# GpSimd in the mixing stage: decay products, probability normalisation and one weight cast per layer

## The chip, the cores and the metric

The kernel runs on one core of one Trainium2 chip. The metric is device time in microseconds, the median of several runs. Engines are named as in the profile: PE is TensorE, DVE is VectorE, ACT is ScalarE, POOL is GpSimd, SP is SyncE, which issues most of the DMAs.

## The reference

Two layers of a decoder trunk over 256 tokens of width 1024, in f32. A layer is half a SwiGLU, a mixing step with three branches, another half SwiGLU and a per-layer embedding; a norm ends the program. The change lies in mixing:

```
u  = rmsnorm(h);  u @ w_in is split among three branches and three gates
A) sparse attention:   logits = q . c_sel * 64**-0.5, masked to the top 64 keys of each query
                       probs  = softmax(logits);  out = probs @ c_sel @ w_uv
B) pooling mixer:      trailing means over 2/4/8/16 tokens minus the token itself, a 128x128 map per group
C) SSD, 2 chunks of 128 tokens, 16 heads in 2 groups:
                       L      = exp(segsum(A))                      (decay within a chunk)
                       y_diag = (C_l . B_s * L[l, s]) @ X           per head
                       ... states, y_off, skip, gate, norm
h += (sum_b sigmoid(gate_b) * (branch_b @ w_b)) @ w_out
```

## The kernel before

Weights come in units of 128 x 1024 f32, each stored so that eight 128 x 128 blocks follow each other. SP loads a unit into `raw` (4 buffers), ACT casts it to a high part `whi` (L145; 5 buffers), DVE subtracts to get the low part `wlo` (L146; 5 buffers), and PE multiplies in three passes, high by high, high by low and low by high (L211 to L213), into a PSUM bank named `mm` (products of weight units) or `aux` (everything else). Units are asked for up to four ahead.

In `mix` the branches are Python generators that `weave` interleaves: `states` (the SSD branch), `attend` (attention), `pools` (pooling) and `gate` (the gate projections, which fill PE in between; `U_IN` + 45 is one of their units). A scheduler then orders each engine's instructions by a timeline of its own, so an edit on one engine can move rows on others; engines wait for each other by semaphores, and each runs its queue in order.

The names that matter: `ms` (tile `ct` in the profile) holds the decays of a chunk `h` and a group `g`, 8 heads as two halves of 4 x 128. DVE makes a running sum of the rates (`rates`, loaded by DMA to tile `gh`) with a scan (L1099), ACT takes the exponential (L1104), for `h == 0` DVE copies the last column to `e0` (L1107), and L1108 multiplies by `cb` (tile `gl`), the product of B and C that all heads of a group share. `near` (helper line L111) multiplies the result with X on PE. In `softmax`, `ps` holds the logits of 4 heads x 128 keys (`h == 0`, one pair of tiles) or 2 heads x 256 keys (`h == 1`, two calls with a pair each); DVE adds the mask and finds the maximum (L921), ACT takes the exponential and its sum (L923), DVE the reciprocal (L925), ACT multiplies each head by its own (L927), PE transposes `pr` (tile `t2`, helper line L114), ACT copies the transposed tile (L939). In `pool_group`, DVE adds shifted copies (L1168, L1169), corrects the start (L1173), takes the mean minus the token (L1176), ACT casts to a high part (L1181) and DVE, or GpSimd for the third group, subtracts for the low part (L1183). GpSimd also scales X by dt (L1085), masks the index scores (L893) and, at the end of the program, scales a gain (L1258). L260 is the low part of a scaled split, and L1031 a step of dt.

Of the kernel before, what the change touches and what calls it, by code (L numbers as in the profile page):

```python
# [13 lines left out]
OP = mybir.AluOpType  # L14
AX = mybir.AxisListType

P = 128
# [38 lines left out]
U_IN = U_KV + 2  # L56
# [12 lines left out]
class Builder:  # L69
# [71 lines left out]
    def load(self, layer, u, n, keep=False):  # L141
        nc = self.nc
        raw, hi, lo = self.parts()
        nc.sync.dma_start(raw[:, :n], self.ins["w"][layer, u, :, :n])
        nc.scalar.copy(hi[:, :n], raw[:, :n])  # L145
        ins = nc.vector.tensor_tensor(lo[:, :n], raw[:, :n], hi[:, :n].bitcast(F), op=OP.subtract)  # L146
        if keep:
            self.tc.keep_in_program_order(ins)
        self.turn(ins)
        return hi, lo  # L150
# [757 lines left out]
    def softmax(self, h, two, mb, out):  # L908

        nc = self.nc  # L910
        nb = h + 1
        nk = nb * P
        per = 512 // nk
        prs = []
        for ps, _ in two:
            pr = self.t([P, per, nk])
            mx = self.t([P, per], tag="mx", bufs=2)
            sums = self.t([P, per], tag="sum", bufs=2)
            for j in range(per):
                x = mx[:, j:j + 1]  # L920
                nc.vector.tensor_tensor_reduce(pr[:, j], ps[:, j * nk:(j + 1) * nk], mb[:, :nk],  # L921
                                               1.0, 3.0e38, OP.add, OP.min, accum_out=x)
                self.last = nc.scalar.activation(pr[:, j], pr[:, j], AF.Exp, bias=x, scale=-1.0,  # L923
                                                 accum_out=sums[:, j:j + 1])
            nc.vector.reciprocal(sums, sums)  # L925
            for j in range(per):
                nc.scalar.mul(pr[:, j], pr[:, j], sums[:, j:j + 1])  # L927
            prs.append(pr)
            yield
        for _ in range(4 - h):  # L930
            yield
        pts = [self.bank("aux") for _ in prs]
        for pt, pr in zip(pts, prs):
            for j in range(4):
                self.transpose(pt[:, j * P:(j + 1) * P],
                               pr[:, j // nb, (j % nb) * P:(j % nb + 1) * P], self.ident)
        for (_, heads), pt in zip(two, pts):
            th = self.t([P, 4, P])
            nc.scalar.copy(th, pt.rearrange("p (a b) -> p a b", a=4))  # L939
            out.append((heads, th))  # L940
            yield
# [63 lines left out]
    def ssd(self, layer, sm, xs, xt, bc, cb, zs, room):  # L1005
        nc = self.nc
# [53 lines left out]
        def rate(*key):  # L1060
            i = wanted.index(key)
            for k in wanted[i:i + 3]:
                if k not in rates:
                    rates[k] = fetch(*k)
            return rates[key]
# [26 lines left out]
        for g in range(2):  # L1092
            gs = slice(g * 4, (g + 1) * 4)
            for h in range(2):
                ms = self.a([P, 2, 4, P], F, "ct")
                for q in range(2):

                    m = ms[:, q]
                    nc.vector.tensor_tensor_scan(m.rearrange("p a b -> p (a b)"),  # L1099
                                                 rate(g, h, q).rearrange("p a b -> p (a b)"),  # L1100
                                                 self.after.rearrange("p a b -> p (a b)"),
                                                 0.0, OP.add, OP.mult)
                    yield
                    self.last = nc.scalar.activation(m, m, AF.Exp)  # L1104
                    if h == 0:
                        k = g * 8 + q * 4
                        nc.vector.tensor_copy(e0[:, k:k + 4], m[:, :, P - 1])  # L1107
                    nc.vector.tensor_tensor(m, m, cb[:, h, g, None].to_broadcast([P, 4, P]),  # L1108
                                            op=OP.mult)
                    yield  # L1110
                ps = self.bank("aux")

                def near():
                    for j in range(8):
                        b, k = (j % 2) * 64, j // 2
                        self.mm(ps[b:b + 64, k * P:(k + 1) * P],
                                         xt[:, h, g * 8 + j], ms[:, j // 4, j % 4],
                                         start=True, stop=True)

                yield  # L1120
                yield
                yield near
                yk = y[:, gs, h * P:(h + 1) * P]
                nc.vector.tensor_tensor(yk, yk, ps.rearrange("p (a b) -> p a b", a=4), op=OP.add)
                yield

            x0 = self.t([P, 8, 64])
            nc.vector.tensor_tensor(x0, xt[:, 0, g * 8:(g + 1) * 8],
                                    e0[:, g * 8:(g + 1) * 8, None].to_broadcast([P, 8, 64]),
                                    op=OP.mult)  # L1130
            po = self.bank("aux")
            e1 = self.t([P, 4, P])
            x = rate(g, 1, 2)
            for j in range(4):
                nc.vector.tensor_tensor_scan(e1[:, j], x[:, j], self.ones, 0.0, OP.add, OP.mult)
            self.last = nc.scalar.activation(e1, e1, AF.Exp)
            yield
            yield
            for j in range(4):
                a = x0[:, 2 * j:2 * j + 2].rearrange("p a b -> p (a b)")  # L1140
                self.mm(po[:, j * P:(j + 1) * P], a, cb[:, 2, g], start=True, stop=True)
            yield
            nc.vector.tensor_tensor(e1, po.rearrange("p (a b) -> p a b", a=4), e1, op=OP.mult)
            yk = y[:, gs, P:]
            nc.vector.tensor_tensor(yk, yk, e1, op=OP.add)
            yield
            if g == 0:
                ysh, ysl = [], []
            ysh.append(self.a([P, 4, S], FR, "a4", 7))
            ysl.append(self.a([P, 4, S], FR, "a4", 7))  # L1150
            for i in range(4):
                k = g * 4 + i
                nc.vector.tensor_tensor(y[:, k], y[:, k], zs[:, k], op=OP.mult)
                self.square(k, y[:, k])
                self.split_scaled(ysh[g][:, i], ysl[g][:, i], y[:, k],
                                  self.col(layer, "ssd_norm", k))
                yield
# [336 lines left out]
```

## Time and profile before

| what | before |
|---|---|
| median of 3 runs | 1299.63 us (1299.38 to 1300.03) |
| the profiled execution | 1300.84 us, of which the span of instructions is 1299.1 us |
| PE busy | 1290.3 us (99%) |
| DVE busy | 1046.3 us (81%) |
| ACT busy | 739.5 us (57%) |
| POOL busy | 17.9 us (1%), 27 instructions |
| mixing of layer 0, woven part | about 290 to 370 us |
| mixing of layer 1, woven part | about 935 to 1015 us |

Busy time of PE counts from a matmul's start to its modelled end, and matmuls overlap; a wait shows as a gap between starts. In the views below a row of the timeline is start, duration, engine, line, operation, result and inputs by the program's names; a group's row ends with busy time, the mean in ns and idle time before it. Line numbers are those of the kernel before; in the changed kernel they are 3 higher from L146 on up to the normalisation and 2 higher behind it.

### The profile page before, as it was taken

To read this page: it belongs to the slowest core of one execution; us is meant where nothing else is said; L and a number is where in the kernel's file an instruction comes from. 1 tells how busy PE (TensorE), PEld (TensorE's weight loads), DVE (VectorE), ACT (ScalarE), POOL (GpSimd) and SP (SyncE) were. 2 spreads that over 40 slices of the span, in tenths; PEclk is the share of its full clock that TensorE was granted. 3 is DMA by queue.
4 is the path that set the end of the run, shared out by engine and by line. 5 is a ranking of instruction groups with operands and counts; after the bars stand their busy time and mean duration, and the time that the engine had idled before them with its cause. 6 is when DMAs were issued, how large, how long until landed. Compare 5 with 4: busy or idle time off the path is not lost.

```text
span 1299.1 us, 28286 instructions
## 1 busy us (share of the span) xinstructions
PE 1290.3 (99%) x11398; PEld 1282.0 (99%) x11398; DVE 1046.3 (81%) x1935; ACT 739.5 (57%) x1209; POOL 17.9 (1%) x27
## 2 busy tenths in 40 slices
PE   9999999999999999999999999999999999999998
PEld 9999999999999999999999999999999999999998
DVE  7877669987999887766997776799879989777667
ACT  6644446666874555544654444476667646544455
POOL 0000000000000000000000000000100000000000
PEclk9999999999999999999999999999999999999999
DMA  7766646586647576666556665556965566655661
GB/s 251 247 193 195 194 158 211 179 222 205 188 142 235 162 227 194 195 191 194 188 195 194 194 196 191 162 192 184 212 224 165 183 199 211 197 195 193 194 194 66
DMA packets 89571, 250.51 MB, mean 193 GB/s; under 512 B 25184, under 2 KB 27872, under 8 KB 89440
## 3 DMA queue, kind: packets, MB, share of 16 engines
q1 hardware_dynamic: 89008, 247.92, 60.6%
q8 instruction: 89, 1.46, 0.5%
q10 hardware_dynamic: 432, 0.79, 0.2%
q14 instruction: 42, 0.34, 0.1%
HBM read 245.50 MB, written 1.08 MB: 190 GB/s over the span
## 4 chain that ended last, share of the span: by engine, by line
PE 87%; DVE 7%; ACT 2%; DMA 2%; issue 2%; DVEq 0%; SPq 0%; ACTq 0%
PE mm L213 27%; PE mm L212 27%; PE mm L211 27%; DVE wlo L146 2%; DVE ct L1099 1%; PE aux L111 1%; ACT whi L145 1%; DMA gh<-rates 1%; DMA raw<-in_w_dram 1%; PE mm L230 1%; PE mm L227 1%; PE aux L213 1%; PE aux L212 1%; ACT t L923 1%; PE mm L225 1%
## 5 line engine op out<-in xcount | busy, mean ns | idle before, releaser
L145 ACT CAST whi<-raw 128x1024 fp32r<-128x1024 f32 (+1 forms) x456 | 475.1, 1045 | 484.9 <-PE mm L212 353.8
L146 DVE TENSOR_TENSOR wlo<-raw,whi 128x1024 fp32r<-128x1024 f32 (+1 forms) x456 | 552.2, 1215 | 170.1 <-ACT whi L145 162.2
L212 PE MATMUL mm<-ul,whi 128*128 128x256 f32 x2438 | 672.0, 276 | 0.0
L213 PE MATMUL mm<-uh,wlo 128*128 128x256 f32 x2438 | 671.8, 277 | 0.0
L211 PE MATMUL mm<-uh,whi 128*128 128x256 f32 x2402 | 662.3, 277 | 0.8 <-ACT whi L145 0.8
L212 PEld LDWEIGHTS mm<-ul,whi 128*128 128x128 f32 x2438 | 457.5, 188 | 0.1
L213 PEld LDWEIGHTS mm<-uh,wlo 128*128 128x128 f32 x2438 | 457.0, 188 | 0.2
L211 PEld LDWEIGHTS mm<-uh,whi 128*128 128x128 f32 x2402 | 449.8, 188 | 2.1 <-ACT whi L145 1.2
L213 PE MATMUL mm<-gh,wlo 128*128 128x256 f32 x704 | 194.1, 276 | 0.0
L212 PE MATMUL mm<-gl,whi 128*128 128x256 f32 x704 | 194.1, 276 | 0.0
L211 PE MATMUL mm<-gh,whi 128*128 128x256 f32 x704 | 193.7, 276 | 0.0
L213 PEld LDWEIGHTS mm<-gh,wlo 128*128 128x128 f32 x704 | 132.2, 188 | 0.0
L212 PEld LDWEIGHTS mm<-gl,whi 128*128 128x128 f32 x704 | 132.2, 188 | 0.0
L211 PEld LDWEIGHTS mm<-gh,whi 128*128 128x128 f32 x704 | 131.9, 188 | 0.0
L212 PE MATMUL mm<-a,whi 128*128 128x256 f32 x256 | 70.7, 276 | 0.0
L213 PE MATMUL mm<-a,wlo 128*128 128x256 f32 x256 | 70.7, 276 | 0.0
L211 PE MATMUL mm<-a,whi 128*128 128x256 f32 x256 | 70.7, 276 | 0.0
L213 PEld LDWEIGHTS mm<-a,wlo 128*128 128x128 f32 x256 | 48.1, 188 | 0.0
L211 PEld LDWEIGHTS mm<-a,whi 128*128 128x128 f32 x256 | 48.1, 188 | 0.0
L212 PEld LDWEIGHTS mm<-a,whi 128*128 128x128 f32 x256 | 48.1, 188 | 0.0
L498 DVE TENSOR_TENSOR t<-mm,rs_r 128x256 f32<-128x256 f32 x88 | 37.3, 424 | 13.2 <-PE mm L213 13.0
L499 DVE TENSOR_TENSOR t<-t,mm 128x256 f32<-128x256 f32 x87 | 36.5, 420 | 2.6
(300 smaller groups left out, 1271.1 us busy)
## 6 DMA issues: line engine op xcount, KB each, us to landing
raw<-in_w_dram SPq DMA_DIRECT2D x446, 512.0 KB, 4.3
gh<-rates SPq DMA_DIRECT2D x16, 256.0 KB, 4.1
raw<-in_w_dram SPq DMA_DIRECT2D x8, 352.0 KB, 3.0
ul<-a SPq DMA_DIRECT2D x32, 64.0 KB, 4.8
a<-in_x_dram SPq DMA_DIRECT2D x3, 512.0 KB, 5.3
gh<-rates SPq DMA_DIRECT2D x8, 128.0 KB, 4.5
a<-in_x_dram SPq DMA_DIRECT2D x1, 544.0 KB, 3.7
raw<-in_w_dram SPq DMA_DIRECT2D x2, 256.0 KB, 4.4
```

The costliest lines, as they stand in the source:

```text
L111: self.tc.keep_in_program_order(self.nc.tensor.matmul(*args, **kw))
L145: nc.scalar.copy(hi[:, :n], raw[:, :n])
L146: ins = nc.vector.tensor_tensor(lo[:, :n], raw[:, :n], hi[:, :n].bitcast(F), op=OP.subtract)
L211: (self.mm if keep else mm)(ps, a[0], b[0], start=start, stop=False)
L212: mm(ps, a[0], b[1], start=False, stop=False)
L213: mm(ps, a[1], b[0], start=False, stop=stop)
L225: (self.mm if keep and k == 0 else mm)(ps, w[0][:, s], u[0][:, k], start=k == 0, stop=False)
L227: mm(ps, w[0][:, s], u[1][:, k], start=False, stop=False)
L230: mm(ps, w[1][:, k * P:(k + 1) * P], u[0][:, k], start=False, stop=k == last)
L498: ins = [nc.vector.tensor_tensor(t, p1[0], r, op=OP.mult), nc.vector.tensor_tensor(g, t, p1[1], op=OP.mult)]
L499: nc.vector.tensor_tensor(g, t, p1[1], op=OP.mult)]
L923: self.last = nc.scalar.activation(pr[:, j], pr[:, j], AF.Exp, bias=x, scale=-1.0, accum_out=sums[:, j:j + 1])
```

## The change

Three pieces of mixing go to GpSimd. The decay products change their engine and keep their shape (128 x 512). The normalisation becomes one product of 128 x 512 with the reciprocals broadcast along the keys, for each tile of probabilities, in place of one ACT instruction per head. And one weight unit per layer, `U_IN` + 45, is cast on GpSimd.

```diff
@@ load
         nc.sync.dma_start(raw[:, :n], self.ins["w"][layer, u, :, :n])
-        nc.scalar.copy(hi[:, :n], raw[:, :n])
+        if u == U_IN + 45:
+            nc.gpsimd.tensor_copy(hi[:, :n], raw[:, :n])
+        else:
+            nc.scalar.copy(hi[:, :n], raw[:, :n])
@@ softmax
             nc.vector.reciprocal(sums, sums)
-            for j in range(per):
-                nc.scalar.mul(pr[:, j], pr[:, j], sums[:, j:j + 1])
+            nc.gpsimd.tensor_tensor(pr, pr, sums[:, :, None].to_broadcast([P, per, nk]), op=OP.mult)
             prs.append(pr)
@@ ssd
                         nc.vector.tensor_copy(e0[:, k:k + 4], m[:, :, P - 1])
-                    nc.vector.tensor_tensor(m, m, cb[:, h, g, None].to_broadcast([P, 4, P]),
+                    nc.gpsimd.tensor_tensor(m, m, cb[:, h, g, None].to_broadcast([P, 4, P]),
                                             op=OP.mult)
```

The scheduler's order changes with it. On GpSimd the following stood before from layer 0's product with dt on (`ul_541` and `t1_683` belong to mixing of layer 0, `gl_1585` and `ul_1780` to layer 1):

```order
L1085 TENSOR_TENSOR ul_541_3872<-ul_541_3872,dt_547_3902 128x512 x4
L1183 TENSOR_TENSOR t1_683_4786<-t1_681_4783,t1_682_4785 128x256
L893 AFFINE_SELECT gl_1585_11072<-gl_1585_11072 128x128 x2
L1085 TENSOR_TENSOR ul_1780_12469<-ul_1780_12469,dt_1786_12499 128x512 x4
L1258 TENSOR_SCALAR idxw_2450_17030<-idxw_2450_17030 128x256
```

Now its queue reads as follows behind the same product of layer 0 (`ct_589` and `ct_610` are decays of the first group, `ct_669` and `ct_691` of the second, chunk 0 ahead of chunk 1; `t2_601` to `t2_704` tiles of probabilities, `whi_613` the unit's high part):

```order
L1110 TENSOR_TENSOR ct_589_4170<-ct_589_4170,gl_346_2475 128x512 x2
L1110 TENSOR_TENSOR ct_610_4314<-ct_610_4314,gl_346_2475 128x512 x2
L146 CAST whi_613_4323<-raw_612_4322 128x1024
L929 TENSOR_TENSOR t2_601_4268<-t2_601_4268,sum_603_4270 128x512
L929 TENSOR_TENSOR t2_607_4301<-t2_607_4301,sum_609_4303 128x512
L1110 TENSOR_TENSOR ct_669_4709<-ct_669_4709,gl_346_2475 128x512 x2
L929 TENSOR_TENSOR t2_647_4564<-t2_647_4564,sum_649_4566 128x512
L929 TENSOR_TENSOR t2_657_4614<-t2_657_4614,sum_659_4616 128x512
L1185 TENSOR_TENSOR t1_683_4778<-t1_681_4775,t1_682_4777 128x256
L1110 TENSOR_TENSOR ct_691_4845<-ct_691_4845,gl_346_2475 128x512 x2
L929 TENSOR_TENSOR t2_692_4849<-t2_692_4849,sum_694_4851 128x512
L929 TENSOR_TENSOR t2_704_4897<-t2_704_4897,sum_706_4899 128x512
```

Every decay product, every normalisation and the cast of layer 0 stand in one queue, the pooled group's subtraction among them.

PE at the last softmax of layer 0 (`aux_718` takes the first tile's transposes, `aux_719` the second's, `mm_714` is a gate projection, `mm_721` the fourth pooled group), before:

```order
L212 MATMUL mm_714_4970<-ul_389_2714,whi_678_4746 128x256
L213 MATMUL mm_714_4970<-uh_388_2713,wlo_679_4747 128x256
L211 MATMUL mm_714_4970<-uh_388_2713,whi_678_4746 128x256
L114 MATMUL aux_718_4989<-ident_75,t2_692_4857 128x128 x2
L212 MATMUL mm_714_4970<-ul_389_2714,whi_678_4746 128x256
L213 MATMUL mm_714_4970<-uh_388_2713,wlo_679_4747 128x256
L114 MATMUL aux_718_4989<-ident_75,t2_692_4857 128x128 x2
L211 MATMUL mm_714_4970<-uh_388_2713,whi_678_4746 128x256
L212 MATMUL mm_714_4970<-ul_389_2714,whi_678_4746 128x256
L114 MATMUL aux_719_4990<-ident_75,t2_704_4906 128x128 x2
L213 MATMUL mm_714_4970<-uh_388_2713,wlo_679_4747 128x256
L114 MATMUL aux_719_4990<-ident_75,t2_704_4906 128x128 x2
```

and now:

```order
L214 MATMUL mm_714_4960<-uh_388_2713,whi_678_4738 128x256
L215 MATMUL mm_714_4960<-ul_389_2714,whi_678_4738 128x256
L216 MATMUL mm_714_4960<-uh_388_2713,wlo_679_4739 128x256
L114 MATMUL aux_718_4979<-ident_75,t2_692_4849 128x128 x4
L214 MATMUL mm_714_4960<-uh_388_2713,whi_678_4738 128x256
L215 MATMUL mm_714_4960<-ul_389_2714,whi_678_4738 128x256
L216 MATMUL mm_714_4960<-uh_388_2713,wlo_679_4739 128x256
L114 MATMUL aux_719_4980<-ident_75,t2_704_4897 128x128 x4
L214 MATMUL mm_721_4991<-t1_708_4924,whi_531_3753 128x256
L214 MATMUL mm_714_4960<-uh_388_2713,whi_678_4738 128x256
```

The first tile's four transposes come four rows of `mm_714` earlier and stand together, the second tile's follow after three rows, and the fourth pooled group's first matmul comes right behind them, where it stood 19 rows of `mm_714` behind the first transposes.

PE at the cast unit of layer 0 (`mm_629` uses `whi_613`, `mm_633` is the second pooled group, of which `t1_623` is the high and `t1_624` the low part), before:

```order
L213 MATMUL mm_629_4427<-uh_388_2713,wlo_593_4200 128x256
L211 MATMUL mm_629_4427<-uh_388_2713,whi_613_4329 128x256
L212 MATMUL mm_629_4427<-ul_389_2714,whi_613_4329 128x256
L211 MATMUL mm_633_4458<-t1_623_4396,whi_531_3753 128x256
L211 MATMUL mm_634_4464<-uh_388_2713,whi_597_4233 128x256
L114 MATMUL aux_625_4412<-ident_75,t2_601_4268 128x128
L212 MATMUL mm_634_4464<-ul_389_2714,whi_597_4233 128x256
```

and now:

```order
L216 MATMUL mm_629_4421<-uh_388_2713,wlo_593_4200 128x256
L214 MATMUL mm_633_4452<-t1_623_4390,whi_531_3753 128x256
L215 MATMUL mm_633_4452<-t1_624_4391,whi_531_3753 128x256
L216 MATMUL mm_633_4452<-t1_623_4390,wlo_532_3754 128x256
L214 MATMUL mm_634_4458<-uh_388_2713,whi_597_4233 128x256
L215 MATMUL mm_634_4458<-ul_389_2714,whi_597_4233 128x256
```

The unit's first use moves behind the pooled group and 16 more rows, and the whole pooled group is asked for where the unit stood.

## The prediction, as put on record before the run

> **What bounds the kernel now.** I read the page's engine row first, then the list of what TensorE waits for, then the groups of instructions that the change moves, then the windows of 10 us through mixing, and at last the timeline of GpSimd beside VectorE.
>
> ```profile
> PE 1290.3 (99%) x11398; PEld 1282.0 (99%) x11398; DVE 1046.3 (81%) x1935; ACT 739.5 (57%) x1209; POOL 17.9 (1%) x27
> PE mm L211 <- ACT whi L145: 0.8, 2, 0.5
> PE aux L114 <- ACT t L927: 0.8, 2, 0.4
> L1108 DVE TENSOR_TENSOR ct<-ct,gl 128x512 f32<-128x512 f32 x16 | 11.1, 691 | 0.1
> L927 ACT ACTIVATE t<-t,sum 128x256 f32<-128x256 f32 x16 | 7.0, 499 | 0.0
> L927 ACT ACTIVATE t<-t,sum 128x128 f32<-128x128 f32 x16 | 4.9, 395 | 0.0
> L145 ACT CAST whi<-raw 128x1024 fp32r<-128x1024 f32 x446 | 467.9, 1051 | 475.9 <-PE mm L212 349.9 <-DMA raw<-in_w_dram 48.1 <-ACT t L339 23.9
> 330.00:340.00 10.00, 10.00 (x108) 9.57 (x107) 10.00 (x21) 6.66 (x13) 0.00 (x0) 1.00 0.76 231
> 340.00:350.00 10.00, 10.00 (x91) 10.00 (x90) 9.97 (x27) 10.00 (x26) 0.00 (x0) 1.00 0.52 151
> ```
>
> TensorE sets the time. It is busy for 99% of the span, and after its first instruction the whole program has it waiting 0.8 + 0.8 = 1.6 us, twice for a weight cast (L145) and twice for a normalisation (L927). Three of the four lie in mixing (below; the other L145, of 0.5 us, stands near 847 us, ahead of layer 1's mixing). About 1.6 us is therefore all that the change can win, while results that come later than TensorE asks for them can cost more than that. In the windows the figures behind the length are busy us of TensorE, its weight loads, VectorE, ScalarE and GpSimd: from 330 to 350 us, inside mixing of layer 0, VectorE has no free time and GpSimd does nothing.
>
> **What a GpSimd instruction costs VectorE.** The next rows put GpSimd instructions beside the VectorE instructions that ran at the same time (start, duration).
>
> ```profile
> 266.62 0.29 POOL L893 TENSOR_SCALAR_AFFINE_SELECT gl<-gl 128x128 f32<-128x128 f32 x1 [30.74 <-DVE gl L889]
> 234.50 1.22 DVE L146 TENSOR_TENSOR wlo<-raw,whi 128x1024 fp32r<-128x1024 f32 x1
> 234.72 1.15 POOL L893 TENSOR_SCALAR_AFFINE_SELECT gl<-gl 128x128 f32<-128x128 f32 x1 [232.10 <-DVE gl L889]
> 289.27 0.19 DVE L1030 SCALAR_TENSOR_TENSOR dt<-dt_y,dt_x 128x32 f32<-128x32 f32 x1
> 289.38 1.23 DVE L146 TENSOR_TENSOR wlo<-raw,whi 128x1024 fp32r<-128x1024 f32 x1
> 289.60 1.91 POOL L1085 TENSOR_TENSOR ul<-ul,dt 128x512 f32<-128x512 f32 x1 [22.69 <-DMA raw<-in_w_dram]
> 290.52 1.03 DVE L1031 SCALAR_TENSOR_TENSOR da<-dt,al 128x32 f32<-128x32 f32 x1
> 291.81 0.68 DVE L256 TENSOR_TENSOR a<-aux,a 128x512 fp32r<-128x512 f32 x1
> 292.47 1.04 POOL L1085 TENSOR_TENSOR ul<-ul,dt 128x512 f32<-128x512 f32 x1
> 293.48 1.04 POOL L1085 TENSOR_TENSOR ul<-ul,dt 128x512 f32<-128x512 f32 x1
> 936.63 1.04 POOL L1085 TENSOR_TENSOR ul<-ul,dt 128x512 f32<-128x512 f32 x1
> 937.17 1.58 DVE L146 TENSOR_TENSOR wlo<-raw,whi 128x1024 fp32r<-128x1024 f32 x1 [1.37 <-ACT whi L145]
> ```
>
> The same select takes 0.29 us alone and 1.15 us when it starts inside an L146. A product of 512 takes 1.04 us, but 1.91 us when it starts inside an L146. It goes the other way too: L1031 takes 1.03 us while a product runs, where L1030, of the same size, had taken 0.19 us; an L146 that starts inside a product takes 1.58 us for 1.22. L256, which reads one of its inputs from PSUM, keeps 0.68 us beside a running product. So the two engines exclude each other for the length of an instruction where VectorE's has both inputs in SBUF. I price a GpSimd product at 1.0 us (from 292.47 to 293.48) plus its wait for the VectorE instruction in front. Who goes first when both wait is read from L1031: it ended at 291.55, before the next product could have run, so I let them take turns.
>
> The Trainium skill, page "SBUF — State Buffer", section "SBUF: two separate sides", calls this an exclusive lock that is held for the whole instruction, and counts every VectorE instruction with two SBUF inputs; by that rule the scans (L1099) and the short sums (L1169, L1176) are shut out as well, which no row here shows by itself.
>
> **The change part by part.** Per layer, eight decay products leave VectorE (at most 8 x 0.69 = 5.5 us) and take 8 x 1.0 on GpSimd. Sixteen normalisations leave ScalarE ((7.0 + 4.9) / 2 = 6.0 us) and become six products, 6 x 1.0. One cast (1.05 us) leaves ScalarE. No row shows it on GpSimd: a product reads as many elements in 1.0, and the following row, one input of 256, gives 4 x 0.86 = 3.4. Eight selects of 128 would be 8 x 0.29 = 2.3; I take 2.3, since a select too reads one input of one pass, and keep 1.0 and 3.4 as ends.
>
> ```profile
> L1258 POOL TENSOR_SCALAR idxw<-idxw 128x256 f32<-128x256 f32 x1 | 0.9, 856 | 27.7 <-DMA idxw<-in_gn_dram 27.7
> 308.81 0.69 DVE L1108 TENSOR_TENSOR ct<-ct,gl 128x512 f32<-128x512 f32 x1
> 312.42 0.32 PE L111 MATMUL aux<-ct,ul 128*64 128x128 f32 x1
> 321.18 0.69 DVE L1108 TENSOR_TENSOR ct<-ct,gl 128x512 f32<-128x512 f32 x1
> 332.10 1.09 PE L111 MATMUL aux<-ct,ul 128*64 128x128 f32 x16
> 338.35 1.25 SPq L1053 DMA_DIRECT2D gh<-rates  x2
> ```
>
> GpSimd thus takes on about 16 us per layer and can shut VectorE out that long, which gets 5.5 back. Much of it is hidden. The first chunk's products end at 309.5 now and are read at 312.4, the second chunk's end at 321.9 and are read at 332.1: 2.9 and 10 us of cover, against an L146 in front (1.2) and the longer product (0.3); with the cover gone TensorE would wait by the difference. On SP one rate load of layer 0 goes behind one weight load; rate loads are issued some 15 us ahead of their scan (338 for 355), so that is nothing unless the weight load itself waits as long. In layer 1 L1258 now stands ahead of the first normalisations; the wait for its data ended with 965, about where those become ready, so nothing. Two places remain. The first is the last softmax of each layer, shown for layer 0:
>
> ```profile
> 357.25 0.13 DVE L1168 COPY t<-gl 128x1 f32<-128x1 f32 x1
> 357.30 0.43 DVE L1169 TENSOR_TENSOR t<-gl 128x271 f32<-128x271 f32 x1
> 357.64 0.42 DVE L921 CUSTOM_DVE_ANT_0 t<-aux,idxw 128x256 f32<-128x256 f32 x1
> 361.04 0.16 DVE L925 RECIPROCAL sum<-sum 128x2 f32<-128x2 f32 x1
> 363.47 0.42 DVE L1176 SCALAR_TENSOR_TENSOR t<-t,gl 128x256 f32<-128x256 f32 x1
> 360.95 0.28 PE L211 MATMUL mm<-uh,whi 128*128 128x256 f32 x1
> 361.29 0.28 PE L211 MATMUL mm<-uh,whi 128*128 128x256 f32 x1
> 361.95 0.33 PE L114 MATMUL aux<-ident,t 128*128 128x128 f32 x1 [0.38 <-ACT t L927]
> ```
>
> TensorE starts a matmul of 256 every 0.113 us (three from 360.95 to 361.29), so the 0.66 up to 361.95 hold a stall of 0.55. In the changed order the transposes stand four matmuls earlier, due at 360.95. The second scan leaves VectorE at 357.25. The first decay product, its exponential done, has the lock until 358.25, L1169 follows until 358.6, the second product runs until 359.6. The four L921 begin at 358.6 instead of 357.64, 0.95 late, and the exponentials with them. Two L1108 (1.2) no longer stand behind, so the reciprocal comes out even, at 360.9. GpSimd then waits for the next L1169 (0.35) and multiplies from 361.25 to 362.3: TensorE stalls 362.35 - 360.95 = 1.4. The second reciprocal stands behind an L1169 that is shut out until 362.2 and ends at 362.65; the short sum and L1176 go first, the product ends at 364.15. TensorE is there at 363.13 (four transposes 0.44, three matmuls 0.34) and stalls 1.0. The pooled group's low part waits for L1176, the lock and an L146, until 365.6, and is due at 365.15: 0.5. In all 2.9 for 0.55 now: +2.35 per layer, +4.7 for two, since layer 1 runs through the same lines with the same wait (two of them make the 0.8).
>
> The second place is the moved cast, in layer 0:
>
> ```profile
> 318.44 0.43 DVE L1169 TENSOR_TENSOR t<-t 128x270 f32<-128x270 f32 x1
> 323.46 0.19 ACT L923 ACTIVATION_READ_ACCUMULATOR t<-t,mx 128x1 f32 x1
> 324.46 0.28 PE L213 MATMUL mm<-uh,wlo 128*128 128x256 f32 x1
> 325.00 0.39 PE L211 MATMUL mm<-uh,whi 128*128 128x256 f32 x1 [0.27 <-ACT whi L145]
> ```
>
> The stall 325.00 - 324.46 - 0.113 = 0.43 goes: the cast can run on GpSimd from 320.7, behind two decay products, to 323.0, and its unit is now asked for some 20 rows later, near 327. But L1169 is shut out for 0.95 by a decay product, so the exponentials end at 324.4 instead of 323.6, and the pooled group behind them on ScalarE and VectorE (0.5, 0.4, 0.4) is now asked for at once, at 324.57: stalls of 0.76 and 0.4. Net +0.7. In layer 1 TensorE doesn't wait at this place today, so there the chain has more time; between 0 and +0.7 I take 0. The middle softmax is the nearest other spot: between nothing and +0.7 per layer, taken as nothing because its products queue only behind two decay products.
>
> Sum: 4.7 + 0.7 = +5.4 us of span. The profiled execution took 1300.84 with a span of 1299.1, 1.2 above the median of 1299.63; a difference is what I worked out, so it goes on the median: 1305.0 us.
>
> **Rivals.**
> - Not slower: the lock falls where nobody waits. If L1169 isn't shut out, or VectorE's other slack takes it, L921 isn't late, the two stalls of today go and nothing replaces them: between -1.6 and +1.4, 1298.0 to 1301.0. For it speaks that TensorE never waits for a low part today; against it the full windows and the transposes due 0.45 us earlier at a place that stalls already. It turns at L921: up to 0.3 late it holds.
> - VectorE becomes the bound. If products go twice in a row (+1.0 per layer), the cast takes 3.4 (+1.1 to +1.4 per layer) and the middle softmax adds 0.7, that is 2 x 3.1 more: +11.6, 1311. For it the 16 us against 5.5; against it that TensorE reads several weight units behind VectorE.
> - Faster by over 0.2% (2.6 us, about what can be told from no change) would take more than all of TensorE's waits.
>
> The Trainium skill, page "GPSIMD Engine Reference", section "Engine selection", puts work with one input at roughly line rate; by an estimate from its clock the cast takes 0.9 us, below my lower end, no run here shows it, and the sum would stay, as the cast is hidden either way.
>
> **How the numbers follow.** The lock at the two places has 0.64, not slower 0.25, VectorE as the bound 0.09, faster 0.02. The forecast's lower end (if the pooled group isn't late) comes below +2.6, so 0.04 goes to "same": 0.29. The range runs from 1299.0, which leaves out the lower third of the first rival, to 1311.0, the worked end of the second.
>
> **What would show it.** L921 of the last softmax about 1 us later behind its scans; GpSimd products of 1.0 us alone and up to 2.2 beside L146; L146's mean above 1215 ns; waits of TensorE at L114 that name GpSimd, 1 us and more, twice per layer. If these stay below 0.5, the low end is right; if TensorE waits for wlo, the high end. The forecast is wrong where GpSimd's products don't wait for VectorE's two-input work.

## The result and the profile after

The change made the kernel slower: 1308.04 us, median of 5 runs (1307.22 to 1309.68), against 1299.54 us before (1299.38 to 1300.03, 5 runs). That is 8.5 us, a ratio of 1.0067 (95% interval 1.0053 to 1.0080). The profiled execution took 1309.68 us with a span of 1307.9 us, 8.8 us more than the span before.

The page of the changed kernel, its engine row and its list of TensorE's waits (us in total, times, longest):

```profile
PE 1294.0 (99%) x11398; PEld 1283.9 (98%) x11398; DVE 1055.6 (81%) x1919; ACT 727.7 (56%) x1175; POOL 60.4 (5%) x57
PE aux L114 <- POOL t L929: 4.6, 6, 1.3
PE mm L215 <- POOL t L1185: 1.0, 2, 0.8
PE mm L215 <- DVE t L1185: 0.6, 2, 0.4
PE mm L214 <- ACT t L1183: 0.2, 1, 0.2
```

The waits of 1.6 us (L145, L927) are gone, and 6.4 us stand in their place, 4.6 of them for the new normalisation on GpSimd. ScalarE lost 11.8 us of work and VectorE gained 9.3 us, although sixteen products of 0.69 us had left it. Two groups show where most of VectorE's time went, and the others what GpSimd's instructions took (busy, mean ns):

```profile
L1155 DVE TENSOR_TENSOR uh<-uh,gl 128x256 f32<-128x256 f32 x16 | 10.0, 682 | 0.1
L1171 DVE TENSOR_TENSOR t<-gl 128x271 f32<-128x271 f32 x8 | 7.6, 950 | 0.0
L1110 POOL TENSOR_TENSOR ct<-ct,gl 128x512 f32<-128x512 f32 x16 | 25.8, 1627 | 68.7 <-DVE e L1109 51.7 <-ACT ct L1106 16.7
L929 POOL TENSOR_TENSOR t<-t,sum 128x512 f32<-128x512 f32 x12 | 14.9, 1254 | 5.1 <-DVE sum L928 5.1
L146 POOL CAST whi<-raw 128x1024 fp32r<-128x1024 f32 x2 | 2.1, 1037 | 0.0
```

L1155, the same line as L1153 before, had a mean of 420 ns and L1171 (L1169 before) of 435 ns. Both have two SBUF inputs, and both now hold waiting time. The products wait as well: 1627 and 1254 ns where one alone takes 1.04 us.

The last softmax of layer 0 after, from the timeline (start, duration); its rows before are in the prediction:

```profile
357.75 2.33 DVE L1101 TENSOR_TENSOR_SCAN ct<-gh,after 128x512 f32<-128x512 f32 x2
359.77 2.86 POOL L1110 TENSOR_TENSOR ct<-ct,gl 128x512 f32<-128x512 f32 x2 [1.95 <-ACT ct L1106]
360.05 1.42 DVE L1171 TENSOR_TENSOR t<-gl 128x271 f32<-128x271 f32 x1
361.40 0.41 DVE L924 CUSTOM_DVE_ANT_0 t<-aux,idxw 128x256 f32<-128x256 f32 x1
363.56 0.28 PE L216 MATMUL mm<-uh,wlo 128*128 128x256 f32 x1
363.59 0.15 DVE L928 RECIPROCAL sum<-sum 128x2 f32<-128x2 f32 x1
363.82 1.22 POOL L929 TENSOR_TENSOR t<-t,sum 128x512 f32<-128x512 f32 x1 [1.19 <-DVE sum L928]
364.25 0.82 DVE L1170 COPY t<-t 128x8 f32<-128x8 f32 x1
365.10 0.65 PE L114 MATMUL aux<-ident,t 128*128 128x128 f32 x4 [1.26 <-POOL t L929]
365.83 0.28 PE L216 MATMUL mm<-uh,wlo 128*128 128x256 f32 x1
366.65 0.99 PE L114 MATMUL aux<-ident,t 128*128 128x128 f32 x4 [0.55 <-POOL t L929]
```

L1171 takes 1.42 us for 0.43, so L924 starts 1.0 us later behind it. The two decay products take 2.86 us: twice 1.04, 0.31 until the scan ends at 360.08, and about 0.43 for the L1171 that went between them. So the scans shut GpSimd out too, and the engines take turns; the row for the copy L1170 (0.82 us, where that copy had a mean of 0.18 before) shows that a copy with one SBUF input waits as well, while L924, with one input from PSUM, keeps 0.41. The Trainium skill, "SBUF — State Buffer", section "SBUF: two separate sides", counts just these: VectorE instructions with two SBUF inputs, and those in a two-port mode, which it says plain f32 copies use; the trace agrees. TensorE stalls by 365.10 - 363.56 - 0.113 = 1.42 us and by 366.65 - 365.83 - 0.113 = 0.71 us.

Behind these stalls stands something that the prediction does not have. In the windows the third figure from the end is the granted TensorE clock:

```profile
364.00:366.00 2.00, 0.90 (x7) 0.81 (x7) 1.78 (x6) 1.29 (x3) 1.49 (x2) 1.00 0.00 0
366.00:368.00 2.00, 1.46 (x7) 1.17 (x7) 2.00 (x3) 1.03 (x2) 0.60 (x1) 0.71 0.04 8
368.00:370.00 2.00, 2.00 (x12) 2.00 (x11) 1.99 (x4) 2.00 (x5) 0.00 (x0) 0.50 0.46 117
370.00:372.00 2.00, 2.00 (x18) 2.00 (x18) 2.00 (x6) 2.00 (x4) 0.00 (x0) 0.94 0.73 229
```

After the two stalls the clock falls to half for about 3 us. The time lost is 2 x (0.29 + 0.50 + 0.06) = 1.7 us. It appears in no list of waits: TensorE counts as busy. This execution is the slowest of the five, with a mean granted clock of 0.998; the one at the median has 0.999, so the median may hold less of this loss.

### The profile page after: what moved, and what is told of

It reads as the page before. It is cut to its first block, busy times and chain, and to the rows that moved or that the text cites. A ratio compares the mean times of both kernels' runs of the same rounds, so it can differ in the third digit from the quotient of the medians.

```text
span 1307.9 us, 28291 instructions
## 1 busy us (share of the span) xinstructions
PE 1294.0 (99%) x11398; PEld 1283.9 (98%) x11398; DVE 1055.6 (81%) x1919; ACT 727.7 (56%) x1175; POOL 60.4 (5%) x57
## 4 chain that ended last, share of the span: by engine, by line
PE 91%; DVE 5%; ACT 2%; DMA 1%; issue 1%; POOL 0%; DVEq 0%; ACTq 0%; POOLq 0%
PE mm L215 28%; PE mm L216 28%; PE mm L214 28%; PE aux L111 2%; DVE wlo L149 1%; DVE ct L1101 1%; PE aux L216 1%; PE aux L215 1%; ACT whi L148 1%; PE aux L214 1%; DVE t L1171 1%; ACT t L926 1%; PE mm L233 1%; PE mm L230 1%; PE mm L228 1%
## 5 line engine op out<-in xcount | busy, mean ns | idle before, releaser
L149 DVE TENSOR_TENSOR wlo<-raw,whi 128x1024 fp32r<-128x1024 f32 (+1 forms) x456 | 553.0, 1218 | 166.3 <-ACT whi L148 158.2
L896 POOL TENSOR_SCALAR_AFFINE_SELECT gl<-gl 128x128 f32<-128x128 f32 x4 | 2.9, 717 | 810.2 <-DVE gl L892 810.2
```

## The experiments

The ratios below are each to the kernel before, timed beside the variant on the same chip in 18 to 21 runs (medians 1300.49, 1300.41 and 1300.26 us for the three groups of experiments). They ask three things: what each part costs alone, whether exclusion or the new order makes the loss, and whether it stays where it is.

### One part at a time

`decay_only` moves only L1108, `norm_only` only L927, `cast_only` only the cast. `norm_dve` has the single product of the normalisation, but on VectorE:

```diff
-            for j in range(per):
-                nc.scalar.mul(pr[:, j], pr[:, j], sums[:, j:j + 1])
+            nc.vector.tensor_tensor(pr, pr, sums[:, :, None].to_broadcast([P, per, nk]), op=OP.mult)
```

> Only the sixteen decay products on GpSimd. Theory (GpSimd and VectorE exclude each other for the length of an instruction where VectorE's has two SBUF inputs, and what comes late is the maximum and exponential of the last softmax): L921 of the last softmax leaves about 1 us later, normalisation stays on ScalarE in quarters, so TensorE's wait for it grows from 0.55 to about 1 to 2 us per layer: 1301 to 1304 us. Rival A (the loss comes from the normalisation alone, one product that has to be whole before any transpose): within 0.5 us of before. Rival B (the loss comes from the new order on TensorE): as far as the order differs from before here, it is small, so within 1 us of before.

> Only the normalisation on GpSimd, twelve products for 32 ScalarE instructions. Theory: each product takes 1.0 us plus its wait for VectorE where two ScalarE instructions took 0.9, and VectorE's pooled sums wait in turn; TensorE's waits at the transposes become about 1 us and 0.5 us per layer: 1301 to 1304. Rival A (the normalisation is the whole loss): 1306 to 1308. Rival C (GpSimd's queue is the loss, decay products ahead of normalisations): within 1 us of before.

> Only one weight cast per layer on GpSimd. Theory: the wait of 0.43 us at the cast of layer 0 goes and nothing else is shut out for long, but the order on TensorE changes with it: 1299.0 to 1300.3. Rival B (the new order on TensorE is the loss): 1301 or more, since the order changes about as much as in the whole change.

> The normalisation as one product per tile, but on VectorE. GpSimd as before. Theory: no instruction is shut out; the product takes 0.7 us in VectorE's queue, which is full there, so TensorE waits about as long as before or up to 1 us longer per layer: 1299 to 1302. Rival A (one product for all heads instead of one per head is the loss, wherever it runs): 1303 to 1307.

| kernel | median, us | ratio (95%) | difference, us |
|---|---|---|---|
| decay_only | 1303.01 | 1.0020 (1.0011 to 1.0030) | +2.5 |
| norm_only | 1305.87 | 1.0041 (1.0029 to 1.0054) | +5.4 |
| cast_only | 1303.34 | 1.0024 (1.0014 to 1.0033) | +2.9 |
| norm_dve | 1310.82 | 1.0078 (1.0064 to 1.0092) | +10.3 |

The decay products came out as the theory had it. The normalisation is dearer than its range, 1305.87 us where 1301 to 1304 were expected, and only 0.1 us short of rival A's; but `decay_only`, which leaves the normalisation alone, loses too, so it is not the whole loss. The cast alone went against the theory and into the range of its rival, the new order. `norm_dve`, with nothing new on GpSimd, lost more than the whole change, and more than its rival allowed. The longest waits of `cast_only` and `norm_dve`, and beside them rows of `cast_only` at the last softmax:

```profile
PE aux L114 <- ACT t L930: 3.6, 2, 1.8
PE mm L211 <- ACT t L1180: 6.1, 2, 3.0
356.62 1.19 DVE L149 TENSOR_TENSOR wlo<-raw,whi 128x1024 fp32r<-128x1024 f32 x1
358.16 0.68 DVE L1111 TENSOR_TENSOR ct<-ct,gl 128x512 f32<-128x512 f32 x1
358.76 0.41 DVE L924 CUSTOM_DVE_ANT_0 t<-aux,idxw 128x256 f32<-128x256 f32 x1
359.21 0.51 ACT L926 ACTIVATE t<-t,mx 128x256 f32<-128x256 f32 x1 [1.48 <-DVE mx L924]
359.72 0.50 ACT L926 ACTIVATE t<-t,mx 128x256 f32<-128x256 f32 x1
360.21 1.04 ACT L148 CAST whi<-raw 128x1024 fp32r<-128x1024 f32 x1
361.16 0.50 ACT L926 ACTIVATE t<-t,mx 128x256 f32<-128x256 f32 x1
```

In `cast_only` VectorE's new order has a low part (L149) and a decay product between the scans and L924, which starts 2.1 us after VectorE is through with the scans (356.62 to 358.76) where it was 0.4 us (357.25 to 357.64). So the first exponential starts at 359.21 where it started at 358.11, and TensorE waits 1.9 us at the transposes, some 40 us behind the moved cast. ScalarE's next weight cast also moved, from behind the fourth exponential to behind the second, but it stands ahead of the normalisation in both kernels.

In `norm_dve` the pooled group's mean (L1175 there) went behind both scans, and TensorE waits 3.0 us for its cast. Neither of these waits is for GpSimd or for the product itself, so rival A doesn't explain them either. The clock adds to `norm_dve`: it falls to half behind both waits, which by the windows costs 1.7 us in each layer. Its twelve products also put 8.1 us (mean 685 ns) on VectorE, so not all of its loss is order.

In `cast_only` the moved cast itself takes 1.04 us and TensorE does not wait for it there: the scheduler's new order costs by itself, and a loss of a few us does not show that the moved instruction is to blame.

### Exclusion without any change of order

`junk_mul` is the kernel before with products on GpSimd whose result nobody reads; `junk_set` does fills there instead. On TensorE, VectorE, ScalarE and SP the rows of both are those of the kernel before:

```diff
                     nc.vector.tensor_tensor(m, m, cb[:, h, g, None].to_broadcast([P, 4, P]), op=OP.mult)
+                    for z in range(2):          # junk_mul
+                        jk = self.t([P, 2, P], mybir.dt.bfloat16, tag="junk", bufs=1)
+                        nc.gpsimd.tensor_tensor(jk, m[:, 2 * z:2 * z + 2], cb[:, h, g, None].to_broadcast([P, 2, P]), op=OP.mult)
...
+                    nc.gpsimd.tensor_copy(jk[:, 0, :1], m[:, 0, :1])      # junk_set
+                    for z in range(4):
+                        nc.gpsimd.memset(jk, 0.0)
```

> The kernel before, with two more products of 128 x 256 on GpSimd behind each decay product (which stays on VectorE). They read the decays from SBUF and write a tile that nobody reads; the order on every other engine is that of the kernel before, word for word. Exclusion theory: L1169 and the second L1108 of the last softmax are shut out for about 0.6 us each, the reciprocal behind them comes late, TensorE's wait at its transposes grows from 0.55 to 1.2 to 2.5 us: 1.3 to 4 us above before. Rival (order and queues are the loss, the engines don't hurt each other): within 0.5 us of before.

> The same place and a similar GpSimd time, but with one copy of 128 x 1 (so that it starts when the decays are there) and four fills of 128 x 256, which read nothing from SBUF. Orders of the other engines as before, word for word. If the exclusion holds only against a GpSimd instruction that reads SBUF: within 0.7 us of before. If any GpSimd instruction shuts VectorE out: 1.3 to 4 us above, like the products.

`junk_mul` took 1309.68 us, a ratio of 1.0071 (1.0058 to 1.0083), 9.3 us above before; `junk_set` 1300.51 us, 0.9999 (0.9991 to 1.0008). Their GpSimd groups, and two of the waits that `junk_mul` has:

```profile
L1112 POOL TENSOR_TENSOR junk<-ct,gl 128x256 bf16<-128x256 f32 x32 | 38.2, 1194 | 84.4 <-DVE ct L1108 35.9 <-DVE sum L925 28.3 <-DVE t L1176 18.4
PE mm L211 <- ACT whi L145: 3.8, 3, 1.8
PE mm L212 <- POOL t L1186: 1.4, 2, 0.9
L1113 POOL MEMSET junk<- 128x256 bf16 x64 | 19.9, 311 | 3.6
L1111 POOL CAST junk<-ct 128x1 bf16<-128x1 f32 x16 | 9.4, 591 | 84.2 <-DVE ct L1108 35.6 <-DVE e L1107 31.0 <-DVE t L1177 17.1
```

Nobody waits for the junk, and no other engine's order moved. Nor is it GpSimd's queue: L1186, for which TensorE waits, found GpSimd idle for 9.9 us in both layers, waiting for its input from ScalarE. So the 9.3 us are exclusion and what it sets off (the clock among it, below). The expected 1.3 to 4 counted one place per layer; the trace shows waits at the cast, the third and fourth pooled group and the last softmax of both layers. The fills kept GpSimd busy for 19.9 us and cost nothing: it is not GpSimd's being busy that hurts, but its reading SBUF. The Trainium skill, "SBUF — State Buffer", section "SBUF: two separate sides", says that a two-input VectorE instruction is shut out only against a GpSimd instruction that reads SBUF; these two runs agree, with 9.3 us against 0.1.

### Asking later, and one VectorE wait less

`after_late4` is the whole change with one more step of the weave ahead of the transposes of the softmaxes with 256 keys (`h == 1`); `before_late4` the kernel before with the same:

```diff
-        for _ in range(4 - h):
+        for _ in range(4 if h == 0 else 4):
             yield
```

> The whole change, and one more step of the weave ahead of the transposes of the softmaxes with 256 keys, so that TensorE is asked for the last ones 27 rows (3.0 us) and for the middle ones 12 rows (1.4 us) later than in the changed kernel. Theory that the loss stands at these transposes, where the products come 1 to 2 us too late, and in the clock that falls after them: the waits of 1.4, 0.7 and 0.9 us go, and about 4 to 6 of the 8.5 us with them: 3 to 4.5 us above before, what is left being the waits at the pooled groups. Rival (VectorE is the bound, and what is saved at one place is waited at the next): 7 to 9 us above before.

> The kernel before with the same extra step of the weave and nothing on GpSimd; the last transposes are asked for 20 rows (2.3 us) later. Theory: the waits of 0.55 us per layer at them go and nothing replaces them: 0.5 to 1.1 us below before. Rival: the later transposes push the values and what follows back, and something else waits: at or above before.

`after_late4` took 1311.52 us, a ratio of 1.0080 (1.0067 to 1.0094), 11.1 above: the rival was right, and somewhat more than right. The waits at the transposes are gone from its list, and in their place stands the fourth pooled group, whose mean L1178 sits in VectorE's queue behind everything that was shut out:

```profile
PE mm L214 <- ACT t L1183: 6.8, 4, 2.8
365.91 1.15 DVE L1178 SCALAR_TENSOR_TENSOR t<-t,gl 128x256 f32<-128x256 f32 x1
367.15 0.41 ACT L1183 CAST t<-t 128x256 fp32r<-128x256 f32 x1 [1.68 <-DVE t L1178]
367.60 0.58 PE L214 MATMUL mm<-t,whi 128*128 128x256 f32 x1 [2.79 <-ACT t L1183]
```

So the lateness belongs to VectorE's queue and not to the place where TensorE asks. `before_late4` took 1300.24 us (1.0000, 0.9991 to 1.0009): the 0.55 us waits went and 0.45 us at the pooled groups came, again VectorE.

`after_e0act` moves the copy to `e0` in the whole change to ScalarE:

```diff
-                        nc.vector.tensor_copy(e0[:, k:k + 4], m[:, :, P - 1])
+                        nc.scalar.copy(e0[:, k:k + 4], m[:, :, P - 1])
```

> The whole change with the copy to e0 (L1109) on ScalarE right behind the exponential, so that the decay products of chunk 0 no longer wait for VectorE's queue. The order of the other engines changes in a few rows only. Theory: the middle softmax's products go 2 us earlier and its waits in layer 0 (0.9 and 0.4 us) shrink or go: 6.5 to 8 above before. Rival (it is VectorE that is late at the middle softmax too, whoever starts first): 8 to 9.5 above before.

It took 1306.34 us, a ratio of 1.0050 (1.0037 to 1.0062), 6.1 above, better than expected and 2.4 us better than the whole change by the two differences. The middle softmax of layer 0, whole change first, then `after_e0act`:

```profile
340.87 0.23 DVE L1109 COPY e<-ct 128x4 f32<-128x4 f32 x2
341.20 2.99 POOL L1110 TENSOR_TENSOR ct<-ct,gl 128x512 f32<-128x512 f32 x2 [14.67 <-DVE e L1109]
343.08 4.09 DVE L1155 TENSOR_TENSOR uh<-uh,gl 128x256 f32<-128x256 f32 x4
344.16 2.40 POOL L929 TENSOR_TENSOR t<-t,sum 128x512 f32<-128x512 f32 x2
345.43 0.66 PE L114 MATMUL aux<-ident,t 128*128 128x128 f32 x4 [0.72 <-POOL t L929]
...
339.78 2.55 POOL L1110 TENSOR_TENSOR ct<-ct,gl 128x512 f32<-128x512 f32 x2 [13.35 <-ACT e L1109]
342.29 2.67 POOL L929 TENSOR_TENSOR t<-t,sum 128x512 f32<-128x512 f32 x2
344.36 0.46 PEld L114 LDWEIGHTS aux<-ident,t 128*128 128x128 f32 x4
```

The products no longer wait for VectorE's queue to reach a 0.16 us copy, they start 1.4 us earlier, and the waits of 0.89 and 0.45 us at this softmax are gone. In the whole change the four L1155 took 4.09 us for 1.43, alternating with products. Not all that `after_e0act` gains stands here: the spans of the profiled executions differ by 3.2 us. These two waits make 1.33 of it, the last softmax of layer 1 makes 0.5 (a stall of 0.91 for 1.37), and the clock makes 1.7, since it stayed at 1.00 in `after_e0act`, although the stalls at the last softmax of layer 0 are 1.41 and 0.71 us there as well; elsewhere `after_e0act` loses some 0.3.

### The cast and the parts together

`cast_twice` is the kernel before, with GpSimd casting the unit once more behind ScalarE's cast; `decay_norm` is the change without the cast; `before_e0late` is a try at a faster version, `before_late4` with the `e0` copies on ScalarE.

> The kernel before; the one unit per layer is cast by ScalarE where it was, and then once more by GpSimd over the same tile (the same values), and VectorE and TensorE wait for the second. The order on all engines at the last softmax is that of the kernel before; only the rows around the cast differ. If what cast_only lost (2.9 us, at the last softmax, where ScalarE's next cast now stands between two exponentials) comes from the new order: within 0.7 us of before. If the cast on GpSimd itself is the loss: 2 to 4 us above before.

> The change without the cast. Theory: exclusion at the last and middle softmax stays, so 6 to 9 us above before; the transposes of the first softmax are asked for 20 rows earlier than before, which can add 1 us and more as in norm_only. If the three parts simply add up (2.5, 5.4 and 2.9 alone, 10.8 in all, against 8.5 for the whole), it would be 8 above; if the cast mends something in the whole, 9 or more.

> A try at a version faster than both: the kernel before with the e0 copies on ScalarE and one more step of the weave ahead of the transposes of the softmaxes with 256 keys, nothing new on GpSimd. before_late4 removed the waits of 0.55 us at the transposes and got 0.45 us at the pooled groups, since VectorE was late; eight copies of 0.15 us per layer less on VectorE would take a part of that: 0 to 1 us below before, which these runs may not tell from no change. Rival (ScalarE's casts come later for it): up to 1 us above.

`cast_twice` took 1300.74 us (1.0008, 0.9999 to 1.0016), 0.5 above, at most 2.1 by the interval, where the last softmax keeps its order; so by the medians most of the 2.9 us of `cast_only` came with the new order. The 0.5 us are a balance: in the profiled execution, the slowest of its eleven, a wait of 1.66 us for the second pooled group came and those at the last softmax went. `decay_norm` took 1311.43 us (1.0101, 1.0086 to 1.0116), 11.2 above: dearer than with the cast, because without it TensorE asks for the first softmax's transposes some 20 rows earlier and waits there as well (1.18 us in layer 0, 1.55 and 0.90 in layer 1, by the starts). The parts do not add up: 2.5 + 5.4 for two of them is 7.9. `before_e0late` took 1301.60 us (1.0014, 1.0005 to 1.0023), 1.3 above, so its rival holds, a little past its range, and no version here beats the kernel before.

## Why the prediction was right, and where its size was off

The forecast was 1305.0 us within 1299.0 to 1311.0, slower; measured were 1308.04. By its steps, with the change of TensorE's stalls worked out from its starts as in the prediction (profiled execution against profiled execution):

| step | predicted, per layer 0 / 1 | measured, layer 0 / 1 |
|---|---|---|
| last softmax and fourth pooled group | +2.35 / +2.35 | +1.85 / +2.11 |
| cast, first softmax, second pooled group | +0.7 / 0 | +0.54 / +0.44 |
| middle softmax | 0 / 0 | +1.33 / 0 |
| third pooled group (L1185 on GpSimd) | not in the sum | +0.85 / +0.16 |
| half clock after the stalls | not in the sum | +1.7 / 0 |

These add to 9.0 us; 0.5 less at a wait near 847 us, outside mixing, makes 8.5 of the 8.8 us by which the spans differ.

- **What bounds it, and the exclusion: right.** It is shown by `junk_mul`. L924 came 1.0 us late behind the scans (0.95 was predicted), the first stall was 1.42 us (1.4), the second 0.71 (1.0). The largest term was 4.7 and measured 4.0.
- **The cast's price: wrong, without effect.** 2.3 us was taken; it took 1.04, at the lower end of the bounds (1.0), and it was hidden either way, as said.
- **The middle softmax: the step that failed.** It was put "between nothing and +0.7 per layer" and "taken as nothing because its products queue only behind two decay products". But those wait for the `e0` copy, which stands behind the four L924, and then take turns with four L1155. `after_e0act` shows it: with the copy elsewhere the 1.33 us are gone.
- **The third pooled group: left out.** Its subtraction had always been on GpSimd, 1.22 us at 353.87 where TensorE lost only 0.16. In the changed kernel its input came later and TensorE waited 1.0 us for it.
- **The clock: left out.** The sum priced a stall at its own length. The profiled run paid 1.7 us on top in layer 0 and nothing in layer 1, where the stalls were 1.37 and 0.71. `after_e0act` and `decay_norm` have the stalls of layer 0 within 0.02 us and paid nothing, so this term is partly chance.
- **The rivals.** "Not slower" fell: L924 was 1.0 us late and its turning point was 0.3. "VectorE becomes the bound" was priced at 1311, and 1308.04 lies as near to it as to the forecast. Two of its three conditions failed (the engines took turns, and the cast took 1.04 us for 3.4); the third, the middle softmax, came dearer than its 0.7. In kind it deserved more than its chance of 0.09: L1155 and the pooled groups were late because of VectorE, and `after_late4` shows that its lateness only moves.
- **The range: in part luck.** The two places that the sum priced at 5.4 us measured 4.9; the other 4.0 us of the table stand where the sum had nothing. The time fell inside the range because its upper end was worked from products twice in a row and a slow cast, which did not come.
- **The signs.** L924 came 1.0 us late, and a product took 1.04 us alone and up to 2.20, as said. The waits at L114 that name GpSimd reached 1 us once per layer and not twice. L149, the former L146, has a mean of 1218 ns for 1215, so its mean shows next to nothing of the exclusion.

Not separated: how much of the 8.5 us the new order adds in the whole change. That exclusion alone can cost this much is shown at an unchanged order by `junk_mul`; that a new order costs with one cast per layer moved is shown by `cast_only` (2.9 us), while the 10.3 us of `norm_dve` are order, its products on VectorE and the clock together. In the whole change each of the quoted waits has an instruction that was shut out ahead of it, which is a reading of the trace and no experiment.

## What to carry to other kernels

Work moved to GpSimd is not free where it reads SBUF and VectorE is full: list VectorE's instructions with two SBUF inputs in that stage and count each product as taking its own length away from them. Then look at every place in the stage where a late VectorE result meets TensorE, not only where it stalls today, and read for what the moved instruction itself now queues (a copy of 0.16 us held two products back). When an edit makes a scheduler plan anew, time the edit with the order held, or a single part that has nothing to do with the theory may show the same loss.

## What the runs showed of the hardware

Half clock after short stalls was not expected. `junk_mul` shows it after one stall of 1.94 us, `after_late4` not after one of 2.95 us in layer 1, though it does in layer 0 (windows of `junk_mul`, then of layer 1 of `after_late4`):

```profile
324.00:326.00 2.00, 0.60 (x6) 0.41 (x4) 2.00 (x5) 2.00 (x8) 1.92 (x2) 1.00 0.05 12
326.00:328.00 2.00, 1.62 (x9) 1.61 (x10) 1.96 (x3) 2.00 (x7) 1.92 (x2) 0.77 0.70 250
328.00:330.00 2.00, 2.00 (x11) 2.00 (x10) 0.51 (x2) 2.00 (x6) 0.18 (x1) 0.50 0.56 188
...
1013.00:1015.00 2.00, 0.83 (x7) 0.83 (x8) 2.00 (x3) 1.29 (x3) 0.34 (x1) 1.00 0.02 4
1015.00:1017.00 2.00, 2.00 (x20) 2.00 (x19) 1.78 (x3) 2.00 (x4) 0.00 (x0) 1.00 0.60 184
```

Stall length alone does not decide it: `decay_norm` has stalls of 1.43 and 0.71 us at the last softmax of layer 0, as the changed kernel has there (1.42 and 0.71), and its clock stayed at 1.00. The Trainium skill, "TensorE: Matmul & The Clock Gate", section "Part 1: The HAM clock gate", says that the clock is set by activity in free-running windows of about 3.4 us; that would explain why one stall falls into a window and another does not, and why the five runs of the changed kernel spread over 2.5 us, but no run here shows it. What the runs show against the section "HAM oscillation — how this bites in real kernels", which warns of gaps above about 3.4 us, is that 1.94 us was enough here.
